# An encoder layer's channel mixer: every engine's order written by hand, right operands summed earlier and split in place

## The chip, the cores and the metric

One core of a Trainium2 chip runs one program. The metric is the device time of one execution in microseconds (us); the profile covers one execution, from the first to the last instruction. The engines are PE (TensorE), ACT (ScalarE), DVE (VectorE), POOL (GpSimd) and SP, whose queue carries every DMA of this kernel.

## The reference

A layer over 2,048 tokens of width 1,024, all in float32:

```
h = rmsnorm(x);  proj = h @ w_in                  # 1024 x 2304
out_a = attention with 8 query heads on 2 key heads, QK-norm, rotary
out_b = differential attention, 4 heads, relative-position bias, then per-head rmsnorm
x = x + concat(out_a, out_b) @ w_out              # 1024 x 1024
h = rmsnorm(x)
u = square(relu(h @ w_up))                        # 1024 x 4096
x = x + u @ w_down                                # 4096 x 1024
```

The last three lines are the channel mixer.

## The kernel before

**Precision.** Each matrix operand is split into a float32r cast (hi, on ACT) and the remainder (lo, on DVE) by `split` (L146, L147). A product is three matmuls: hi hi, hi lo, lo hi.

**Seven products for eight.** Up- and down-projection are each cut 2 x 2 and multiplied with seven half-size products. Each product has a left operand (A11, S2, A12, S3, S1, A22, S4) and a right one (B11, T2, B21, T3, T1, T4, B22). The S and T are sums of quarters, made on POOL by `left_sums` (L709 to L712) and `right_sums` (L718 to L721).

**Output projection** (`out_proj`). w_out comes in eight row blocks through a staging pool of two buffers (`wo_raw`) into eight split tiles that stay. Then for eight blocks of 256 tokens (tc): eight pieces `m_raw` of the attention output are loaded, scaled and split, multiplied with w_out (`py`, L677), added to x and stored as x1. Each 128-token tile is normed: a sum of squares on ACT, a power on POOL (L141), a scaling on DVE, eight transposes on PE. The result `h2_f` is stored to `h2_d` in DRAM.

**Up-projection** (`mlp_up`). For each half c of the tokens (two times 512), `h2_d` is read back in four slices, the T are summed and all seven right operands (128 x 4 x 512, hi and lo, 16 KB of a partition each) are split in 28 slices. Then 16 blocks f of w_up: a 1 MB load, four sums, seven splits (`wu_hi`, `wu_lo`), seven products of 12 matmuls (L763) into three PSUM tiles X, Y, Z. Between them stand p1 (a copy of X on ACT, L784; X is added to only after it), the adds u2, u3, c22, c21, c12 on DVE (L773), and relu and square on ACT (L777, L778). Four sums of the results and seven stores to `us_d` end a block. Three of the right operands lie in a pool (`first`) that is open before the output projection, four in a later one.

**Down-projection** (`mlp_down`). For each of seven products i: 16 pieces of w_down are loaded (one to four loads each), summed in place on POOL (L885) and split into 22 buffers; then for eight token blocks b a tile of u (1 MB) is loaded and split in halves, and 48 matmuls (L899) fill one PSUM tile; `finish` adds it to what it belongs to and stores what is done.

**Memory.** Pools of a stage lie in order of opening from the same base, and a tile waits only for the users of its own bytes. In KB of a partition, attention has: pta 12, acc 8, oa 2, v_a 8, Vb 24, th and tl 8, ob 2, Ka (16) and Ka1 (8) 24, Qa and Qa1 16, Kb 24, T 17.5, Qb 8, Sm 48, small ones. The output projection has: `first` 48, m2b 16, x 8, h 8, gain 4, staging 8, m2a 16, m_raw 7, small 5, w_out 64.

**Order.** A planner simulates the program and orders each engine's instructions, the DMAs on SP's queue among them, from their written priority, its costs and when buffers come free. Engines then run that order without overtaking, waiting on semaphores.

Of the kernel before, what the change touches and what calls it, by code (L numbers as in the profile page):

```python
# [18 lines left out]
P = 128  # L19
# [25 lines left out]
def as32(ap):  # L45
    return ap.bitcast(F32)


class Builder:
# [27 lines left out]
    def dram(self, pool):  # L77
# [8 lines left out]
        self.h2_d = pool.tile([NT, P, ND, P], F32, name="h2_d")  # L86
# [495 lines left out]
    def out_proj(self):  # L582
# [3 lines left out]
        with ExitStack() as es:  # L586
# [4 lines left out]
            stage, m2a, mp, sm = pool("ows", 2), pool("om_a", 1), pool("om", 7), pool("osm", 2)  # L591
# [48 lines left out]
            for tc_ in range(8):  # L640
# [26 lines left out]
                for b in range(NB):  # L667
# [25 lines left out]
                    self.dma(self.h2_d[r0 // P], hf)  # L693
# [21 lines left out]
    def right_sums(self, b11, b12, b21, b22, new):  # L715
# [6 lines left out]
        return {"B11": b11, "T2": t2, "B21": b21, "T3": t3, "T1": t1, "T4": t4, "B22": b22}  # L722

    def mlp_up(self, first):
# [3 lines left out]
        H = 512  # L728
        with ExitStack() as es:
            pool = self.pools(es)  # L730
            later = pool("uh", 1)
            rawp, sump, wop, vp = pool("uraw", 2), pool("usum", 4), pool("uw", 8), pool("uv", 15)
            psx, psy, psz = (pool(n, 2, space=PSUM) for n in ("psux", "psuy", "psuz"))
            for c in range(2):
                B = {}
                for i, n in enumerate(self.RIGHT):
                    B[n] = (first if i < 3 else later).tile([P, 2, 4, H], F32R, name=f"hop_{n}")
                for s in range(4):
                    raw = rawp.tile([P, 2, ND, P], F32, name="h_raw", tag="raw")
                    for i in range(2):  # L740
                        self.dma(raw[:, i], self.h2_d[c * 8 + i * 4 + s])
                    new = lambda: sump.tile([P, 4, P], F32, name="h_sum", tag="sum")
                    blk = lambda i, k: raw[:, k, i * 4 : i * 4 + 4, :]
                    ops = self.right_sums(blk(0, 0), blk(0, 1), blk(1, 0), blk(1, 1), new)
                    ts = slice(s * P, (s + 1) * P)
                    for n in self.RIGHT:
                        self.split(B[n][:, 0, :, ts], B[n][:, 1, :, ts], ops[n])
                for f in range(DFF // 256):
                    raw = rawp.tile([P, ND, 256], F32, name="wu_raw", tag="raw")
                    self.dma(raw, ap["w_up"][0, :, f * 256 : f * 256 + 256].rearrange("(j p) f -> p j f", p=P))  # L750
                    new = lambda: sump.tile([P, 4, P], F32, name="w_sum", tag="sum")
                    blk = lambda i, k: raw[:, k * 4 : k * 4 + 4, i * P : i * P + P]
                    ops = self.left_sums(blk(0, 0), blk(0, 1), blk(1, 0), blk(1, 1), new)
                    A = {}
                    for n in self.LEFT:
                        A[n] = wop.tile([P, 4, P], F32R, name="wu_hi"), wop.tile([P, 4, P], F32R, name="wu_lo")
                        self.split(*A[n], ops[n])

                    def product(ps, i, start):
                        (wh, wl), b = A[self.LEFT[i]], B[self.RIGHT[i]]  # L760
                        for j in range(4):
                            for k, (w, h) in enumerate(((wh, 0), (wh, 1), (wl, 0))):
                                nc.tensor.matmul(  # L763
                                    ps, w[:, j, :], b[:, h, j, :], skip_group_check=not start,
                                    start=(start and j == 0 and k == 0), stop=(j == 3 and k == 2),
                                )

                    def v(name):
                        return vp.tile([P, H], F32, name=name, tag="v")

# [186 lines left out]
```

## Time and profile before

| | |
|---|---|
| Runs | 3445.77, 3447.94 and 8364.44 us; median 3447.94 |
| The profiled execution | 3438.99 us, span 3437.2 us |
| PE busy | 3218.0 us, 94% of the span |
| DVE, ACT, POOL busy | 60%, 45%, 49% |
| DMA | 417.25 MB, mean 121 GB/s |
| Granted clock of PE, mean | 0.972 |

Matmuls are pipelined and their ends are modelled, so PE's busy share says where it has work and not how close it is to its peak. The output projection runs from about 1816 to 2050 us, the up-projection to 2777, the down-projection to the end.

### The profile page before, as it was taken

What the parts mean: (1) busy time and instruction counts of PE and PEld (TensorE: products, weight loads), DVE (VectorE), ACT (ScalarE), POOL (GpSimd) and SP (SyncE); (2) the same over time, 40 slices, a digit from 0 to 9 for tenths busy, and PEclk for the clock granted to TensorE, in tenths of its full rate; (3) what the DMA queues carried; (4) which work ended last, traced back from release to release, by engine and by line L of the source; (5) the groups of instructions that cost most, each with busy time, mean ns of one, the idle gap of its engine ahead of it and who ended that gap; (6) DMA issues with size and microseconds to landing.
All of it is one profiled execution on the core that took longest, in us unless ns stands there. A gap on an engine that the chain in (4) does not pass through costs nothing.

```text
span 3437.2 us, 43470 instructions
## 1 busy us (share of the span) xinstructions
PE 3218.0 (94%) x15584; PEld 2448.7 (71%) x15584; DVE 2065.9 (60%) x3826; ACT 1554.2 (45%) x2386; POOL 1689.7 (49%) x942
## 2 busy tenths in 40 slices
PE   7999989999999999999999986999699979999899
PEld 6888866666666666666666865777577758878787
DVE  6545547777777787777854547445644454454542
ACT  4222227666666656666653224444444433222231
POOL 3434436676666666766661116555655543233600
PEclk9999989999999999999998998999899989999999
DMA  6336380032012211111014543554444477565752
GB/s 200 103 105 206 103 224 22 28 86 59 28 34 74 61 31 44 55 40 29 22 44 165 173 150 119 150 145 138 147 138 138 127 269 253 181 231 191 263 194 86
DMA packets 364408, 417.25 MB, mean 121 GB/s; under 512 B 25344, under 2 KB 293760, under 8 KB 354080
## 3 DMA queue, kind: packets, MB, share of 16 engines
q1 hardware_dynamic: 364192, 414.48, 38.4%
q8 instruction: 123, 2.02, 0.2%
q14 instruction: 93, 0.76, 0.1%
HBM read 283.25 MB, written 139.53 MB: 123 GB/s over the span
## 4 chain that ended last, share of the span: by engine, by line
PE 76%; DVE 11%; DMA 6%; ACT 3%; issue 2%; POOL 1%; SPq 1%; ACTq 0%; POOLq 0%; DVEq 0%
PE pd L899 14%; PE psY L763 7%; PE pq L244 7%; PE po_a L549 6%; PE psX L763 5%; PE py L677 5%; PE ps_s L413 5%; PE psZ L763 5%; PE po_b L467 4%; PE ps_a L538 4%; PE pv L244 3%; PE ps_a L539 3%; PE ptb L460 2%; PE ps_m L503 2%; DVE negm L427 2%
## 5 line engine op out<-in xcount | busy, mean ns | idle before, releaser
L542 POOL TENSOR_TENSOR acc<-acc,pta 128x1024 f32<-128x1024 f32 x224 | 534.1, 2385 | 256.2 <-ACT pta L540 251.4
L418 DVE CUSTOM_DVE_ANT_0 Sm<-ps_s,T 128x512 f32<-128x512 f32 x512 | 338.2, 685 | 124.3 <-PE ps_s L413 122.1
L540 ACT ACTIVATE pta<-ps_a 128x512 f32<-128x512 f32 x512 | 292.2, 594 | 216.2 <-PE ps_a L539 203.3
L899 PE MATMUL pd<-wd_hi,u_hi 128*128 128x512 f32 x896 | 351.3, 392 | 32.6 <-ACT u_hi L146 21.0
L506 DVE TENSOR_REDUCE mxa<-ps_m 128x1 f32<-128x512 f32 x512 | 330.0, 683 | 55.4 <-PE ps_m L503 54.7
L438 POOL TENSOR_TENSOR Sm<-Sm 128x2048 f32<-128x2048 f32 x64 | 293.4, 4584 | 137.5 <-ACT Sm L437 137.4
L899 PE MATMUL pd<-wd_lo,u_hi 128*128 128x512 f32 x896 | 351.0, 392 | 4.2 <-DVE wd_lo L147 4.2
L899 PE MATMUL pd<-wd_hi,u_lo 128*128 128x512 f32 x896 | 350.7, 392 | 1.2 <-DVE u_lo L147 1.2
L413 PE MATMUL ps_s<-Kb,Qb 128*128 128x512 f32 x1024 | 306.1, 409 | 2.6 <-DVE mx L418 2.3
L885 POOL TENSOR_TENSOR wd_raw<-wd_raw 128x512 f32<-128x512 f32 x112 | 182.3, 1640 | 256.1 <-DMA wd_raw<-in_w_down 170.6
L429 ACT ACTIVATE Sm<-Sm,negm 128x2048 f32<-128x2048 f32 x128 | 256.6, 2005 | 88.2 <-DVE negm L427 80.5
L549 PE MATMUL po_a<-pta,v_a 128*64 128x512 f32 x1024 | 280.8, 623 | 2.0 <-ACT pta L540 1.8
L146 ACT CAST u_hi<-u_raw 128x1024 fp32r<-128x1024 f32 x112 | 112.2, 1050 | 326.4 <-PE pd L899 324.0
L538 PEld LDWEIGHTS ps_a<-Qa,Ka 128*128 128x128 f32 x512 | 96.3, 188 | 228.3 <-issue 197.1
L538 PE MATMUL ps_a<-Qa,Ka 128*128 128x512 f32 x512 | 234.1, 458 | 16.4 <-DVE vt L147 12.6
L763 PE MATMUL psX<-hop_B,wu_hi 128*128 128x512 f32 x512 | 166.1, 406 | 88.2 <-ACT wu_hi L146 57.2
L763 PE MATMUL psY<-hop_T,wu_hi 128*128 128x512 f32 x768 | 237.0, 390 | 4.3 <-DVE u L773 4.3
L147 DVE TENSOR_TENSOR tl<-ptb,th 128x512 fp32r<-128x512 f32 x256 | 175.4, 685 | 81.5 <-ACT th L146 81.3
L899 PEld LDWEIGHTS pd<-wd_hi,u_hi 128*128 128x128 f32 x896 | 169.5, 189 | 68.8 <-ACT u_hi L146 21.4
L467 PE MATMUL po_b<-th,Vb 128*128 128x256 f32 x1024 | 208.6, 287 | 9.9 <-ACT th L146 9.4
L413 PEld LDWEIGHTS ps_s<-Kb,Qb 128*128 128x128 f32 x1024 | 179.5, 190 | 47.2 <-DVE mx L418 10.7
L503 PE MATMUL ps_m<-Ka,Qa 128*128 128x512 f32 x512 | 200.8, 432 | 5.8 <-DVE mx L418 1.2
(229 smaller groups left out, 7510.9 us busy)
## 6 DMA issues: line engine op xcount, KB each, us to landing
wd_raw<-in_w_down SPq DMA_DIRECT2D x224, 256.0 KB, 5.5
u_raw<-us_d SPq DMA_DIRECT2D x56, 1024.0 KB, 5.2
wu_raw<-in_w_up SPq DMA_DIRECT2D x32, 1024.0 KB, 6.1
us_d<-us SPq DMA_DIRECT2D x128, 256.0 KB, 5.9
us_d<-c SPq DMA_DIRECT2D x96, 256.0 KB, 2.3
Qb<-qkT_d SPq DMA_DIRECT2D x128, 128.0 KB, 3.0
Qa<-qkT_d SPq DMA_DIRECT2D x48, 256.0 KB, 4.8
m_raw<-mix_d SPq DMA_DIRECT2D x96, 128.0 KB, 2.9
```

Of the source, the lines that this page charges most:

```text
L244: nc.tensor.matmul(ps, a[:, j, :], b[:, j, c0 : c0 + n], start=(j == 0 and k == 0), stop=(j == ND - 1 and k == 2),)
L413: nc.tensor.matmul(ps, Q[:, c, i, qb * P : (qb + 1) * P], K[c][:, ks], start=(i == 0), stop=(i == 1))
L418: nc.vector.tensor_tensor_reduce(out=Sm[:, ks], in0=ps, in1=T[t0][:, o - t0 : o - t0 + 512], scale=1.0, scalar=BIGNEG, op0=ALU.add, op1=AL ...
L438: nc.gpsimd.tensor_tensor(Pm[0], Pm[0], Pm[1], ALU.add)
L467: nc.tensor.matmul(po, V[a][:, kb, :], b[:, kk, :], start=(kb == 0 and n == 0), stop=(kb == NT - 1 and n == 2),)
L506: nc.vector.tensor_reduce(mx[:, kk : kk + 1], ps, AX.X, ALU.max)
L538: nc.tensor.matmul(ps, K[:, ks], Q[:, i, :], start=True, stop=False)
L540: ex = nc.scalar.activation(pt[:, i, :], ps, AF.Exp)
L542: nc.gpsimd.tensor_tensor(acc, prev if kb == 1 else acc, pt, ALU.add)
L549: nc.tensor.matmul(po[i * HD : (i + 1) * HD, :], v_a[:, kb, g * HD : (g + 1) * HD], pt[:, i, :], start=(kb == 0), stop=(kb == NT - 1),)
L763: nc.tensor.matmul(ps, w[:, j, :], b[:, h, j, :], skip_group_check=not start, start=(start and j == 0 and k == 0), stop=(j == 3 and k == 2),)
L899: nc.tensor.matmul(ps, a[:, k, :], w, start=(k == 0 and m == 0), stop=(k == NK - 1 and m == 2))
```

## The change

`h2_d` is replaced by two DRAM tensors, one with the quarters of the normed tokens (`hb_d`) and one with their T sums (`ht_d`); the sums are made tile by tile during the output projection (`mlp_sums`), in raw and sum buffers that are now opened before it. A right operand is then one 1 MB load into its lo half, from which hi is cast and in which the remainder is left (`operand`, `in_place`). The staging pool of w_out has one buffer. Up- and down-projection stand under `manual_schedule`: each engine, SP among them, issues in the written order. Within block n of the up-projection the weights of n + 1 are split, those of n + 2 loaded, and block n - 1 is finished. In the down-projection T2 comes third, each piece of it is also stored (`wt_d`), and T4 is taken from that.

```diff
-        self.h2_d = pool.tile([NT, P, ND, P], F32, name="h2_d")
+        self.hb_d = pool.tile([2, 4, P, 4, 512], F32, name="hb_d")
+        self.ht_d = pool.tile([2, 4, P, 4, 512], F32, name="ht_d")
+        self.wt_d = pool.tile([16, P, 512], F32, name="wt_d")
...
-            stage, m2a, mp, sm = pool("ows", 2), pool("om_a", 1), pool("om", 7), pool("osm", 2)
+            stage, m2a, mp, sm = pool("ows", 1), pool("om_a", 1), pool("om", 7), pool("osm", 2)
...
-                    self.dma(self.h2_d[r0 // P], hf)
+                    c, th, s_ = r0 // 1024, (r0 // 512) % 2, (r0 // P) % 4
+                    for dh in range(2):
+                        self.dma(self.hb_d[c, 2 * dh + th, :, :, s_ * P : s_ * P + P], hf[:, dh * 4 : dh * 4 + 4, :])
+                    if th:
+                        self.mlp_sums(c, s_, rawp, sump)
+                if tc_ == 4:
+                    self.first = [self.operand(0, n, first) for n in self.RIGHT[:3]]
...
+    def mlp_sums(self, c, s, rawp, sump):
+        ts = slice(s * P, s * P + P)
+        raw = rawp.tile([P, 4, 4, P], F32, name="h_raw", tag="raw")
+        for i in range(4):
+            self.dma(raw[:, i], self.hb_d[c, i, :, :, ts])
+        new = lambda: sump.tile([P, 4, P], F32, name="h_sum", tag="sum")
+        for i, t in enumerate(self.right_sums(*(raw[:, i] for i in range(4)), new)):
+            self.dma(self.ht_d[c, i, :, :, ts], t)
...
+    def operand(self, c, n, pool, both=True):
+        t = pool.tile([P, 2, 4, 512], F32R, name=f"hop_{n}")
+        src = (self.hb_d if n[0] == "B" else self.ht_d)[c, self.PLACE[n]]
+        self.dma(t[:, 1], src)
+        if both:
+            self.in_place(t)
+        return t
+    def in_place(self, t):
+        self.split(t[:, 0], t[:, 1], as32(t[:, 1]))
...
+            wop, vp, later = pool("uw", 9), pool("uv", 16), pool("uh", 1)
+            es.enter_context(self.tc.manual_schedule())
...
+            load(0)
+            load(1)
+            sums(0)
+            late = self.RIGHT[3:]
+            for i in range(7):
+                wsplit(0, i)
+                if i >= 3:
+                    B[0][self.RIGHT[i]] = self.operand(0, self.RIGHT[i], later)
+            last = 2 * NF - 1
+            coming = []
+            for n in range(last + 1):
+                if n < last - 1:
+                    load(n + 2)
+                if n < last:
+                    sums(n + 1)
+                if n:
+                    finish(n - 1)
+                X, Y, Z = (p.tile([P, H], F32, name=m) for p, m in ((psx, "psX"), (psy, "psY"), (psz, "psZ")))
+                for i in range(7):
+                    product(n, i, (X, Y, X, Y, Z, Y, Z)[i], i in (0, 1, 4))
+                    if i == 0:
+                        p1 = v("p1")
+                        nc.scalar.copy(p1, X)
+                    elif i == 1:
+                        u2 = add("u2", Y, p1)
+                    elif i == 2:
+                        c11 = act(v("c11"), X)
+                    elif i == 3:
+                        u3 = add("u3", Y, p1)
+                    elif i == 4:
+                        c22 = add("c22", Z, u3)
+                        act(c22, c22)
...
+                    if n < last:
+                        wsplit(n + 1, i)
+
+                    if len(coming) > 2 or (coming and n == NF):
+                        self.in_place(coming.pop(0))
+                    if n == NF - 1:
+                        name = self.RIGHT[i]
+                        B[1][name] = self.operand(1, name, first if i < 3 else later, both=False)
+                        coming.append(B[1][name])
...
+        SPARE = 6
+        order = ("B11", "B21", "T2", "T3", "T1", "T4", "B22")
+        terms = {"B11": "+11", "B21": "+21", "T2": "+12-11-22", "T3": "+22-12", "T1": "+12-11", "T4": "+21-00", "B22": "+22"}
...
+            rp, arp, ap_, bhp, keep, blp, xp = (
+                pool("dr", 10), pool("dar", 2), pool("da", 2), pool("dbh", NK + SPARE), pool("dk", 1), pool("dbl", NK + SPARE), pool("dx", 4),
+            )
...
+            def wsplit(i, k):
+                (t, _), *more = raws.pop((i, k))
+                if order[i] == "T2":
+                    (b, _), (c, _) = more
+                    nc.gpsimd.tensor_tensor(t, t, b, ALU.subtract)
+                    nc.vector.tensor_tensor(t, c, t, ALU.subtract)
+                    self.dma(self.wt_d[k], t)
+                elif more:
+                    nc.gpsimd.tensor_tensor(t, t, more[0][0], ALU.subtract)
+                wh, wl = bhp.tile([P, H], F32R, name="wd_hi"), blp.tile([P, H], F32R, name="wd_lo")
+                self.split(wh, wl, t)
+                Bs[i].append((wh, wl))
...
+            AHEAD = 3
+            made = 0
+            def piece():
+                nonlocal made
+                if made + AHEAD < len(pieces):
+                    wload(*pieces[made + AHEAD])
+                if made < len(pieces):
+                    wsplit(*pieces[made])
+                made += 1
+            uload(0)
+            for q in range(AHEAD):
+                wload(*pieces[q])
+            uload(1)
+            usplit(0)
+            for k in range(NK):
+                piece()
+            for m, (i, b) in enumerate(steps):
+                x = x1(i, b)
+                uload(m + 2)
+                usplit(m + 1)
+                for _ in range(1 if 0 < b < 7 else NK - SPARE if b == 7 else 0):
+                    piece()
+                ps = psd.tile([P, H], F32, name="pd")
...
+                finish(i, b, ps, x)
...
-            with tc.tile_pool(name="mh", bufs=1, reuse_waits="tile") as first:
-                self.out_proj()
-                self.mlp_up(first)
+                first, rawp, sump = pool("uf", 1), pool("uraw", 2), pool("usum", 4)
+                self.out_proj(first, rawp, sump)
+                self.mlp_up(first, rawp, sump)
             self.mlp_down()
```

`first`, the raw buffers and the sum buffers take 48, 16 and 8 KB of a partition; `wop` takes 36, `vp` 32 and `later` 64 KB. In the down-projection the pools in their order take 20, 16, 32, 44, 32, 44 and 8 KB.

## Rows read from the trace of the kernel before

**Rows 1.** windows: us, busy (x) of PE, PEld, DVE, ACT, POOL, PEclk, DMA, GB/s

```profile
1820.00:2045.00 225.00, 219.94 (x1065) 180.47 (x1062) 114.74 (x242) 60.37 (x126) 20.94 (x23) 0.95 0.50 167
2445.00:2777.00 332.00, 312.55 (x1342) 253.52 (x1342) 152.77 (x193) 151.75 (x253) 172.50 (x124) 0.98 0.45 133
2800.00:3437.00 637.00, 616.36 (x2686) 507.05 (x2685) 298.14 (x287) 167.55 (x214) 193.44 (x120) 0.98 0.59 207
```

**Rows 2.** chain of waits, two windows of the up-projection: start us, us, what

```profile
2095.30 2.72 PE psY L763 x12
...
2289.96 0.59 ACT p L784
...
2290.60 3.06 PE psX L763 x12
...
2310.98 1.20 PE psX L763 x4
```

**Rows 3.** waits of PE from 2097 to 2420 us: us in total, times, longest

```profile
PE psX L763 <- ACT p L784: 16.2, 14, 2.6
```

**Rows 4.** timeline into the up-projection: start us, us, instruction

```profile
2044.72 0.40 PE L677 MATMUL py<-wo_hi,m_lo 128*128 128x512 f32 x1
...
2052.59 0.32 SPq L55 DMA_DIRECT2D h_d<-h_f  x1
...
2089.00 1.59 POOL L710 TENSOR_TENSOR w_sum<-w_sum,wu_raw 128x512 f32<-128x512 f32 x1
2089.39 1.75 DVE L147 TENSOR_TENSOR wu_lo<-wu_raw,wu_hi 128x512 fp32r<-128x512 f32 x1
```

**Rows 5.** waits of PE from 2420 to 2450 us

```profile
PE psX L763 <- ACT wu_hi L146: 22.2, 1, 22.2
```

**Rows 6.** waits of PE from 2777 to 2800 us

```profile
PE pd L899 <- ACT u_hi L146: 21.0, 1, 21.0
```

**Rows 7.** chain of waits, 1845 to 1860 us: the last wait for w_out

```profile
1853.39 6.64 PE py L677 x28
```

**Rows 8.** one tile's view, the staging buffers of w_out

```profile
L55 SPq DMA_DIRECT2D wo_raw<-in_w_out x8: 333/333/422, 1816.4 to 1842.9; - x8
L146 ACT CAST wo_hi<-wo_raw x8: 1027/1044/1048, 1821.8 to 1847.4; 128x1024 fp32r<-128x1024 f32 x8
L147 DVE TENSOR_TENSOR wo_lo<-wo_raw,wo_hi x8: 1217/1225/1226, 1822.8 to 1848.5; 128x1024 fp32r<-128x1024 f32 x8
...
DMA to landing us min/median/max: 4.0/5.5/6.1
```

**Rows 9.** one line's view, L413, the last readers of Kb

```profile
L413 PE MATMUL ps_s<-Kb,Qb x1024: 387/396/794, 487.6 to 1732.6; 128*128 128x512 f32 x171
```

**Rows 10.** one line's view, L460 from 1780 to 1800 us

```profile
L460 PE MATMUL ptb<-ident,Sm x20: 271/273/274, 1780.6 to 1796.8; 128*128 128x128 f32 x20
```

**Rows 11.** groups of instructions by line, 2097 to 2777 us

```profile
L147 DVE TENSOR_TENSOR wu_lo<-w_sum,wu_hi 128x512 fp32r<-128x512 f32 x126 | 113.1, 898 | 51.1 <-ACT wu_hi L146 51.0
...
L778 ACT ACTIVATE c<-c 128x512 f32<-128x512 f32 x127 | 80.2, 631 | 3.2
...
L146 ACT CAST wu_hi<-w_sum 128x512 fp32r<-128x512 f32 x124 | 77.0, 622 | 163.1 <-PE psZ L763 70.1 <-PE psY L763 66.0 <-PE psX L763 13.8
...
L773 DVE TENSOR_TENSOR c<-psZ,u 128x512 f32<-128x512 f32 x63 | 43.4, 689 | 47.6 <-PE psZ L763 47.6
...
L718 POOL TENSOR_TENSOR h_sum<-h_raw 128x512 f32<-128x512 f32 x4 | 6.1, 1522 | 5.9 <-DVE wu_lo L147 3.8 <-DVE hop_T L147 1.8 <-DMA h_raw<-h_d 0.3
```

**Rows 12.** DMA issues: bytes of one, median us from issue to landing

```profile
h_d<-h_f SPq DMA_DIRECT2D x16, 512.0 KB, 4.8
h_raw<-h_d SPq DMA_DIRECT2D x16, 512.0 KB, 5.0
```

**Rows 13.** DMA packets and rate from 2777 to 2800 us

```profile
DMA packets 5496, 8.10 MB, mean 352 GB/s; under 512 B 389, under 2 KB 2949, under 8 KB 5240
```

**Rows 14.** the page's costliest groups, the nearest cast of 2048 columns

```profile
L429 ACT ACTIVATE Sm<-Sm,negm 128x2048 f32<-128x2048 f32 x128 | 256.6, 2005 | 88.2 <-DVE negm L427 80.5
```

More of the change, by code (lines that the diff above doesn't have):

```diff
@@ L579, in row_sums, with out_proj @@
         nc.vector.reciprocal(l, l)
[L582 removed]
+    def out_proj(self, first, rawp, sump):
         nc, tc, ap = self.nc, self.tc, self.ap
@@ new lines, in wsplit, with product @@
+            def wsplit(n, i):
+                W[n, i] = wop.tile([P, 4, P], F32R, name="wu_hi"), wop.tile([P, 4, P], F32R, name="wu_lo")
+                self.split(*W[n, i], ops[n][self.LEFT[i]])
+            def product(n, i, ps, start):
+                (wh, wl), b = W[n, i], B[n // NF][self.RIGHT[i]]
+                for j in range(4):
+                    for k, (w, h) in enumerate(((wh, 0), (wh, 1), (wl, 0))):
+                        nc.tensor.matmul(
+                            ps, w[:, j, :], b[:, h, j, :], skip_group_check=not start,
+                            start=(start and j == 0 and k == 0), stop=(j == 3 and k == 2),
+                        )
@@ L806, in mlp_down @@
+            finish(last)
     def mlp_down(self):
@@ L827, in rows, with plus, x1 @@
                 return slice(t0, t0 + P)
-            def x1(half, b, dh):
+            def plus(t, a, b):
+                nc.vector.tensor_tensor(t, a, b, ALU.add)
+            goes = {"B21": (0, 0), "T3": (0, 1), "T1": (1, 1), "T4": (1, 0)}
+            def x1(i, b):
+                if order[i] not in goes:
+                    return None
+                half, dh = goes[order[i]]
                 t = xp.tile([P, H], F32, name="x1")
@@ new lines, in finish @@
+            def finish(i, b, ps, t):
+                n = order[i]
+                if n == "B11":
+                    nc.scalar.copy(U[b], ps)
+                    return
+                if n == "T2":
+                    plus(U[b], ps, U[b])
+                    return
+                if n == "T3":
+                    nc.gpsimd.tensor_tensor(y12[b], t, U[b], ALU.add)
+                    plus(U[b], ps, U[b])
+                    return
+                half, dh = goes.get(n, (0, 1))
+                if n == "B22":
+                    t = y12[b]
+                    plus(t, ps, t)
+                else:
+                    plus(t, ps, t)
+                    plus(t, t, U[b])
+                    if n == "T1":
+                        plus(y12[b], ps, y12[b])
+                self.dma(out[0, rows(half, b), dh * H : dh * H + H], t)
```

206 lines of the change are left out of this document (71 added, 135 removed).

## The prediction

> **What bounds the kernel now.** I read the busy times by stretch first, then TensorE's waits, then the chain of waits where TensorE stops. The change touches three stretches: the output projection, the up-projection and the down-projection. In each, TensorE is busy for over nine tenths and no other engine comes near it [rows 1]. So a saved microsecond must be one in which TensorE waits or runs at half clock. One 128x512 group of 12 matmuls takes 2.72 us; a block n of the up-projection has seven, 19.04 us, and each mlp stage has 2,688 matmuls, 609 us at that pace [rows 2].
>
> What the two mlp stages take beyond 609 us lies in five places:
> - Each n takes 20.38 us (2310.98 less 2290.60), 1.34 more than its matmuls [rows 2]. The wait shown is for the copy p1 [rows 3], which stands on ScalarE behind weight casts that wait for a buffer; without it the group X2 can't add to X.
> - From the last matmul of the output projection (2044.72 + 0.40 = 2045.1, E below) to an undisturbed start (2095.30 - 2.72 = 2092.6): 47.5 us. The right operands are read back, summed and split there, and the sums of VectorE and GpSimd run against one another [rows 4].
> - The same between the halves: 22.2 us in one wait, some 25 with what follows [rows 5].
> - Into the down-projection: 21.0 us [rows 6].
> - Inside the down-projection: 637 less 616 busy, about 21 [rows 1], where a right operand's pieces come late.
> A sixth place lies before them: the output projection runs freely only from 1853.39 [rows 7], after eight blocks of w_out have come through two staging buffers.
>
> **The change part by part.** Negative is saved; the profiled execution took 3438.99 us, and the sum is made against that.
>
> 1. Staging of w_out with one buffer. One at a time, a block costs 5.5 us landing, 1.04 cast and 1.22 remainder, 7.8 us; eight would be 62 us, and from 1816.4, the first load now, full flow would begin 25 us later than it does [rows 8]. But the 24 KB of raw and sum buffers now open ahead of the output projection's pools. By the sizes given above, the staging buffer moves from 84 KB (attention's Ka1 and Qa, read to the end of attention) to 108 KB (Kb, last read at about 1733 [rows 9]), and the w_out tiles to 140 to 204 KB (T, Qb, Sm). The last probabilities in Sm are transposed at 1797 [rows 10], and they may hold back about half the blocks. Four blocks at 6.5 us from 1797 end at 1823; with the loads hidden under attention, full flow begins about 1830. I take -20. Ends: -35 (the first token block's matmuls also fit into attention's tail) and +25 (not free early).
>
> 2. The right operands' sums during the output projection. Added: 32 GpSimd sums of 1.5 us [rows 11], 49 us on an engine busy 21 of 225 [rows 1]; 32 stores and 32 loads of 256 KB and 32 stores of sums in 512-byte pieces on SP; three 1 MB operand loads with three in-place splits. What hides them is that TensorE has its own work. What they can delay is the power for a tile's norm, which queues behind up to four sums (6 us), and loads of m_raw behind a read-back on SP. I take +5, ends 0 and +15.
>
> 3. Into the up-projection. The split of 28 slices falls away, but the last tile's path stays: its store is issued at E + 7.5 [rows 4], lands 4.8 us on and is read back in 5.0 [rows 12], and four sums take 6.1 (four by 1.52): E + 23.5. The second w_up block needs that raw buffer. In the written order of SP, the loads of T3, T1, T4 and B22 stand behind it. The last sum's store (256 KB, half of h_d's 4.8 or so) and four operands of 1 MB at 352 GB/s [rows 13], 12 us, put B22's landing at about E + 38. ScalarE's order puts all four in-place casts ahead of p1 of n = 0; the last cast, of 128x2048, takes 2.0 us by the nearest row [rows 14]. So X2 starts about E + 40.6, as if X0 had started at E + 35. Against 47.5 that is -12. Ends: -36 (the planner gives both w_up blocks their buffers before the last tile needs them) and +5.
>
> 4. The steady up-projection. Weight casts now come one n ahead and in step with the products, so I follow the loop that goes through p1: p1 0.6 [rows 2], three groups 8.16, then for Z4, Y5 and Z6 each an add 0.69, relu and square 1.26 and the next cast 0.62 [rows 11], with a remainder (wu_lo) on VectorE ahead of each of the last two adds. That is 16.5 plus two remainders, plus about 0.5 for some 14 handovers of 0.04. With a remainder of 0.90, the mean [rows 11], the loop is 18.8 us, inside 19.04. One row speaks against the mean: a remainder took 1.75 us beside a sum on GpSimd [rows 4], and then the loop is 20.5. I take a period of 19.15, nearest the mean: 31 times 1.23 is -38. Ends: -41 and +4.
>
> The Trainium skill ("SBUF — State Buffer", "Who interferes with whom") says that a VectorE instruction with two inputs in SBUF and a GpSimd one that reads SBUF exclude each other for a whole instruction. The row of 1.75 agrees: it ends 0.55 us behind the sum's end at 2090.59. If every remainder met a sum, this part would give +4 by that rule and not -38; the rival for it is below.
>
> 5. Between the halves. In SP's order the seven operand loads stand behind the stores of finish(14), whose last waits for GpSimd at about 11 us into n = 15, and each needs its product done. Then a loop runs through the step: add 0.69, relu and square 1.26, weight cast 0.62, in-place cast 2.0, in-place remainder (twice the 1.22 of 1024 columns [rows 8], less what is paid once per instruction: 2.3). That is 6.9 against 2.72, 4.2 lost in a step. Seven such steps would lose 29, three 12.5; the first also waits for its load. I take 23 against 25: -2.
>
> 6. Into the down-projection. Raw pieces and u tiles now lie on operands that the last n frees one after another, up to 16 us before its end, so the first splits run beside its products. About 14 of 21 goes; some pieces share bytes with last results still being stored. Ends: -21 and 0.
>
> 7. Inside the down-projection. T2 becomes third, T4 costs two loads less by its kept sum, but the order now loads three pieces ahead where the planner took what it could. At the switch to T2, seven pieces remain: 21 loads, ten stores and one u tile, 9.2 MB, 26 us at 352 GB/s, against 21 us until the last piece is wanted (10.9 of the running step plus 15 x 0.68). VectorE then does the late finish and u remainders before the next step: 8 to 9 lost. The other three sums lose up to 3.5 each. About 19 in place of 21: I take 0, ends -10 and +15.
>
> The sum is -20 + 5 - 12 - 38 - 2 - 14 + 0 = **-81**: 3438.99 - 81 = 3358. The median of the three runs, 3447.94, is 9 us above the profiled time, so I predict **3367 us**.
>
> **Rivals.**
> - *The written order gives the period back.* If VectorE's remainders regularly meet GpSimd's sums, the loop of part 4 is 20.5 us and the wait for p1 stays: 3367 + 42 = 3409. For it: the row of 1.75, and eight sums plus seven remainders in each n; the in-order ScalarE can't run p1 ahead. Against it: the mean of 0.90, with as many sums in each n now. It decides at a remainder of about 1.0, where the loop reaches 19.04.
> - *The staging gain doesn't come.* If the planner doesn't start w_out under attention, part 1 gives +20 and not -20: 3407. For it: the first load is at 1816 now and Sm lives to 1797; against it: m_raw and the sums of squares, whose buffers lie on Kb, already run in attention's tail.
> - *More overlaps than I count.* Parts 1 and 3 at their near ends: 15 and 24 more: about 3328, down to 3315 with part 7.
> - *Slower than before: SP in the output projection.* Each of eight mlp_sums makes SP wait for a store to land (4.8), then a read-back (5.0), then four sums (6.1) before the sums' stores. Where m_raw loads stand behind these, TensorE waits up to 16 us eight times: +128, 3495. It decides once more than 10 us of each is uncovered. For it: one queue carries every load. Against it: seven m_raw buffers cover up to a token block of 22 us, and the planner, not a written order, places these loads.
>
> **How the numbers follow.** A measurement tells 2% from no change, 69 us, so faster means below 3379. Forecast 0.49 (own range 3325 to 3410), period given back 0.16, staging 0.15, more overlap 0.11, slower 0.09. The range 3305 to 3425 leaves out the slow rival and the corners of the others. Below 3379: 0.41 of the forecast, all of the overlap rival, 0.04 of the next two, 0.56. Above 3517 needs the slow rival with a bad part 4 or 7: 0.05. Within 2%: 0.39.
>
> **What would show it.** After the change I look for the first free-running group of the output projection near 1830; X2 of n = 0 about 40 us after its last matmul; a distance of 19.1 to 19.3 between X0 of neighbouring n, and remainders near 0.9; a loss of 17 to 27 us over n = 15 and 16, spread over several waits for hop tiles; under 10 us between the last product of the up-projection and the first of the down-projection; and the largest wait inside that stage at the switch to T2. A period above 20, a first w_out load after 1810, or m_raw waits in the output projection would make it wrong.

## The result, and the profile after

The changed kernel took **3384.99 us** in the median of four runs (3381.86 to 3395.9), the kernel before 3446.86; the ratio is 0.9834 with a 95% interval from 0.9801 to 0.9866, in which a run of the kernel before of 8364.44 us is left out. That is faster by more than the measurement is uncertain, inside the range of 3305 to 3425, and 18 us above the 3367 forecast. It is a gain of 1.7%, so the 2% that "faster" meant was missed: the prediction had given 0.56 to under 3379 and 0.39 to a change within 2%, which came. The profiled execution has a span of 3384.7 us against 3437.2: 52.5 us less, where the sum of the parts said 81.

The stages of the two profiled executions, each from its first or to its last matmul (start: the first product of block n = 1 less 19.04 us; for the kernel before as in the prediction):

| | before | after | change | forecast |
|---|---|---|---|---|
| output projection ends (E; parts 1, 2) | 2045.1 | 2059.6 | +14.5 | -15 |
| E to the undisturbed start (part 3) | 47.5 | 46.1 | -1.4 | -12 |
| start to the last product (parts 4, 5) | 684.8 | 635.2 | -49.6 | -40 |
| to the first matmul of the down-projection (part 6) | 21.0 | 4.8 | -16.2 | -14 |
| down-projection (part 7) | 635.0 | 635.3 | +0.3 | 0 |

The busy times by stretch; columns as in [rows 1]. The first row is the changed kernel's output projection from its 96th matmul on; the second and third are 260 us of steady blocks in the second half of the up-projection, before and after:

```profile
1865.00:2060.00 195.00, 182.17 (x864) 146.89 (x863) 96.84 (x180) 45.29 (x92) 39.60 (x38) 0.97 0.69 219
...
2480.00:2740.00 260.00, 247.85 (x1079) 201.31 (x1078) 117.92 (x153) 121.58 (x203) 139.31 (x102) 1.00 0.48 139
...
2460.00:2720.00 260.00, 260.00 (x1149) 215.29 (x1148) 134.45 (x165) 122.77 (x216) 161.46 (x109) 1.00 0.52 151
```

In the up-projection TensorE is busy for 260.00 of 260 us, where it was for 247.85 before. In the first row it misses 13 us of 195, and the DMA moves 219 GB/s. The chain of waits of the changed kernel shows the pace of the up-projection (start us, us, what):

```profile
2455.32 2.72 PE psX L789 x12
...
2474.36 1.81 PE psX L789 x8
```

From X0 of one block to that of the next are 19.04 us (2474.36 less 2455.32), exactly seven products. The waits of TensorE (us in total, times, longest us) in three stretches: the first half, the step between the halves, and the way into the down-projection:

```profile
PE psX L789 <- ACT p L837: 10.5, 1, 10.5
PE psY L789 <- DVE u L799: 1.6, 1, 1.6
...
PE psZ L789 <- DVE c L799: 7.9, 1, 7.9
PE psX L789 <- ACT p L837: 6.1, 1, 6.1
PE psY L789 <- DVE u L799: 3.7, 2, 2.1
...
PE pd L1001 <- ACT wd_hi L149: 4.8, 1, 4.8
PE pd L1001 <- DVE wd_lo L150: 0.8, 1, 0.8
```

The wait for p1 of [rows 3] is gone from the steady blocks. What is left is one wait for p1 and one for a late sum in the first block of the first half, four waits of 17.7 us in all between the halves, and 5.6 us where [rows 6] had 21.0.

### The profile page after: what moved, and what is told of

It is laid out like the page before. It is cut to its first block, busy times and chain, and to the rows that moved or that the text cites. A ratio compares the mean times of both kernels' runs of the same rounds, so it can differ in the third digit from the quotient of the medians.

```text
span 3384.7 us, 43164 instructions
## 1 busy us (share of the span) xinstructions
PE 3227.7 (95%) x15584; PEld 2459.7 (73%) x15584; DVE 2042.2 (60%) x3800; ACT 1530.4 (45%) x2344; POOL 1631.6 (48%) x894
## 5 line engine op out<-in xcount | busy, mean ns | idle before, releaser
L541 PE MATMUL ps_a<-Qa,Ka 128*128 128x512 f32 x512 | 233.6, 457 | 17.7 <-DVE vt L150 13.6
L470 PEld LDWEIGHTS po_b<-th,Vb 128*128 128x128 f32 x1024 | 173.1, 191 | 44.0 <-ACT th L149 14.7
L1001 PEld LDWEIGHTS pd<-wd_lo,u_hi 128*128 128x128 f32 x896 | 169.5, 189 | 48.9 <-DVE wd_lo L150 14.2
L1001 PEld LDWEIGHTS pd<-wd_hi,u_hi 128*128 128x128 f32 x896 | 169.4, 189 | 46.4 <-ACT wd_hi L149 11.3
```

The lines of the kernel that those rows point to most:

```text
L470: nc.tensor.matmul(po, V[a][:, kb, :], b[:, kk, :], start=(kb == 0 and n == 0), stop=(kb == NT - 1 and n == 2),)
L541: nc.tensor.matmul(ps, K[:, ks], Q[:, i, :], start=True, stop=False)
L1001: nc.tensor.matmul(ps, a[:, k, :], w, start=(k == 0 and q == 0), stop=(k == NK - 1 and q == 2))
```

## The experiments

All edits are to the changed kernel except where the kernel before is named. Seen over the runs that left a stage as it was, the end of the output projection lies between 2057 and 2063 us and the written down-projection between 634 and 640; a difference of under 6 us there isn't read. Before, after and the last row of the table ran several times, the others once. The stage times, in the table's order except that here the up-projection counts from its first matmul (X0), which exists in every order:

| kernel | E | E to X0 | X0 to last product | to next stage | down | span |
|---|---|---|---|---|---|---|
| before | 2045.1 | 41.7 | 690.6 | 21.0 | 635.0 | 3437.2 |
| after | 2059.6 | 29.5 | 651.8 | 4.8 | 635.3 | 3384.7 |
| before, nine weight buffers | 2046.0 | 41.9 | 656.2 | 21.0 | 641.5 | 3410.5 |
| planner in the up-projection | 2063.1 | 38.7 | 634.8 | 3.9 | 638.7 | 3382.9 |
| planner in the down-projection | 2063.3 | 26.3 | 652.9 | 7.0 | 619.1 | 3372.8 |
| half blocks, three staging buffers | 2047.2 | 27.6 | 653.9 | 4.7 | 639.8 | 3377.0 |
| no right sums | 2054.3 | 11.2 | 657.0 | 4.7 | 634.2 | 3365.7 |
| late operands first | 2060.8 | 39.1 | 642.2 | 4.7 | 635.6 | 3386.3 |
| second w_up block last | 2060.6 | 27.6 | 664.1 | 4.7 | 639.0 | 3399.7 |
| first splits after the seventh token block | 2057.5 | 28.7 | 652.4 | 4.6 | 638.7 | 3385.8 |
| first splits at the head of the up-projection | 2062.9 | 27.9 | 655.5 | 6.6 | 637.3 | 3393.8 |
| splits between halves later | 2057.3 | 27.7 | 681.6 | 4.7 | 639.3 | 3414.4 |
| combined | 2054.5 | -0.2 | 642.2 | 3.7 | 647.5 | 3351.5 |
| combined, planner in the down-projection | 2056.2 | -0.2 | 641.5 | 3.7 | 629.2 | 3334.3 |

**What gave the period: the order?** The up-projection without its written order:

```diff
             psx, psy, psz = (pool(n, 2, space=PSUM) for n in ("psux", "psuy", "psuz"))
-            es.enter_context(self.tc.manual_schedule())
```

> The up-projection's written order is left to the planner, all else as in the changed kernel. Theory (the written order, with the weights split one block ahead in step with the products, is what brought a block from 20.4 to 19.04 us): the period goes back to 20.0 to 20.5 with waits for p1, the span grows by 30 to 45 us. Rival (the sums made earlier and the in-place splits did it, the order doesn't matter): the period stays at 19.04 to 19.2 and the span within 12 us.

The rival's numbers held: the steady blocks of the planner's order are 19.04 us apart too, with one wait for p1 from 2120 to 2400 us:

```profile
PE psX L788 <- ACT p L836: 5.9, 1, 5.9
```

My theory fell. From E to the last product the planner even took 673.5 us for the written order's 681.3. Between the halves it waits less (2400 to 2470 us):

```profile
PE psX L788 <- ACT p L836: 2.9, 1, 2.9
PE psZ L788 <- DVE c L798: 1.2, 1, 1.2
```

Its four blocks around the step lose 15.3 us for 25.8; its last two lose 6.9, where the written order loses 0.2. The rival's reason, the earlier sums and the in-place splits, is not shown by this run, and the next one speaks against it.

**Or a buffer?** The changed kernel has nine pairs of buffers for split weights where there were eight. This one edit to the kernel before:

```diff
-            rawp, sump, wop, vp = pool("uraw", 2), pool("usum", 4), pool("uw", 8), pool("uv", 15)
+            rawp, sump, wop, vp = pool("uraw", 2), pool("usum", 4), pool("uw", 9), pool("uv", 15)
```

> The kernel before with one edit: nine buffers instead of eight for the split w_up weights, the planner's order kept. Leaving the changed kernel's order to the planner did not bring the old period back, so the order is not the cause. Theory (the copy p1 waited on ScalarE behind weight casts that waited for a buffer; the ninth buffer lets the cast start): the period falls from 20.4 to 19.0 to 19.5, the up-projection is 27 to 40 us shorter. Rival (the place of the splits in the code, a block ahead and between the products, gives it, by the planner's priorities too): the period stays at 20.2 or more.

The theory held. The chain of waits, from X0 of one block to the next:

```profile
2205.28 2.72 PE psX L763 x12
...
2224.32 2.72 PE psX L763 x12
...
2243.36 2.72 PE psX L763 x12
```

19.04 us (2224.32 less 2205.28, 2243.36 less 2224.32), with the planner's order, the old sums and the old splits. The stage is 34.4 us shorter. Counted by 84 matmuls in the order in which TensorE ran them, 31.8 of these are 24 blocks that took 20.35 to 20.39 us and take 19.04 here, as they do in the changed kernel. One run took 3412.68 us beside 3452.84 for the kernel before. So the ninth buffer is enough in the planner's order; whether the written order would have done it with eight no run shows.

**The output projection: the cast that waits.** From 1860 us to the end of this stage the changed kernel's TensorE has one wait of over 2 us. The timeline of it (start us, us, instruction, in brackets the idle time before and what ended it):

```profile
1985.08 1.90 ACT L149 CAST hop_T<-hop_T 128x2048 fp32r<-128x2048 f32 x1 [8.17 <-DMA hop_T<-ht_d]
1986.88 0.71 ACT L149 CAST m_hi<-m_raw 128x256 fp32r<-128x256 f32 x2
...
1987.33 0.80 PE L680 MATMUL py<-wo_hi,m_hi 128*128 128x512 f32 x1 [6.12 <-ACT m_hi L149]
```

ScalarE stands at the in-place cast of T2 for 8.17 us until its load has landed; the cast of m_raw that TensorE needs is behind it. A first attempt to move it:

```diff
-                    self.first = [self.operand(0, n, first) for n in self.RIGHT[:3]]
+                    self.first = [self.operand(0, n, first, both=False) for n in self.RIGHT[:3]]
+                if tc_ == 6:
+                    for t in self.first:
+                        self.in_place(t)
```

> The three first right operands are still loaded after the fifth token block of the output projection, but cast and left with their remainder only after the seventh. In the changed kernel 48 matmuls near 1990 us took 22.6 us where the kernel before needed 12.6, with one wait of 6.1 us for a cast of m_raw and half clock after it. Theory (an in-place cast stands on ScalarE ahead of that cast and waits for its 1 MB load): the wait is gone, the last matmul of the output projection ends near 2050 instead of 2059.6, the span is 8 to 11 us shorter. Rival (the transfers and the sums themselves, on the queue and on GpSimd, delay m_raw): the last matmul stays within 2 us of 2059.6.

It decided nothing: the planner put the cast in the same place (8.58 us of idle time before it at 1983.24, 6.9 us of wait). The next one writes the splits at the head of the up-projection, which moved the cast on ScalarE (4.89 us of idle time before it at 1985.51):

> The in-place splits of the first three right operands are written at the head of the up-projection; their loads stay after the fifth token block. The planner still puts the casts into the output projection, but that of T2, the one that waited 8.2 to 8.6 us for its load at 1983 us, some fifteen instructions of ScalarE later. Theory (that cast, waiting on the in-order ScalarE, made the wait of 6 to 7 us for m_hi): the 48 matmuls near 1990 us take 13 to 15 us instead of 22.6, the output projection ends near 2050. Rival (m_raw itself comes late): its end stays at 2057 to 2061.

The waits of TensorE from 1860 us to the end of the stage:

```profile
PE py L680 <- ACT m_hi L149: 1.7, 1, 1.7
...
PE pt L166 <- DVE xo L161: 7.3, 3, 4.3
```

The wait for m_hi fell from 6.1 to 1.7 us, and the stage ended at 2062.9, no sooner: other waits, for the normed tile above all, took its place. The theory fell; the rival had the end nearly right, but no row shows its reason, an m_raw that comes late. So a single visible wait wasn't the cost.

**The output projection: the sums.** The sums and their read-back left out, as many bytes stored:

```diff
-                        self.mlp_sums(c, s_, rawp, sump)
+                        for i in range(4):
+                            self.dma(self.ht_d[c, i, :, :, s_ * P : s_ * P + P], hf[:, (i % 2) * 4 : (i % 2) * 4 + 4, :])
```

> The right operands' sums are left out: no read-back and no sums on GpSimd in the output projection; as many bytes of the normed tokens are stored in the sums' place, so the operands' values are wrong and all later work is the same. Theory (the sums and their read-back cost the output projection its 14.5 us over the kernel before, and hold the raw buffers into which w_up is loaded): the output projection ends at 2045 to 2051 instead of 2059.6, and the undisturbed start of the up-projection follows 20 to 30 us behind it instead of 46. Rival (the operand loads and the last tile's norm set both): the end stays above 2055 and the distance above 40.

E came at 2054.3, between the two. But its 96th matmul began late (1871.5; 1865.1 in the changed kernel and in the kernel before). From there to the end it took 182.8 us, against 194.5 with the sums (194.4 to 196.4 in the runs that left this stage as it was) and 180.0 before: by this run the sums and their read-back cost 11.7 of the 14.5 us. The start of the up-projection followed 33.2 us behind E, between the two again. X0 was there at 11.2, so the round trip of the last sums is what holds it up. But then the fourth product waited for a sum on VectorE:

```profile
PE psY L790 <- DVE u L800: 13.6, 1, 13.6
```

What VectorE did before that sum:

```profile
2077.13 0.69 DVE L150 TENSOR_TENSOR wu_lo<-w_sum,wu_hi 128x512 fp32r<-128x512 f32 x1 [9.48 <-DMA ht_d<-h_f]
...
2092.17 0.68 DVE L800 TENSOR_TENSOR u<-psY,p 128x512 f32<-128x512 f32 x1
```

A remainder of the weights waited 9.48 us for a store of `h_f`; by the sizes, the weights' buffers (72 to 108 KB) lie over those of `h_f` (96 to 104 KB). The four in-place remainders came behind it, all ahead of the sum in VectorE's written order. The stores from `h_f` to `ht_d` are this edit's own, so part of the 13.6 us may belong to the experiment.

**Staging.** Half blocks of w_out through three buffers, and not whole blocks through one:

```diff
-            stage, m2a, mp, sm = pool("ows", 1), ...
+            stage, m2a, mp, sm = pool("ows", 3), ...
...
-                raw = stage.tile([P, D], F32, name="wo_raw")
+                for q in range(2):
+                    raw = stage.tile([P, 512], F32, name="wo_raw")
...
```

> The staging of w_out takes half blocks in three buffers (6 KB of a partition) instead of whole blocks in one (4 KB). In the changed kernel two blocks came early, the others were held by attention's last probabilities until 1801 us and then came one at a time, 6 to 7.5 us each, until 1848; the kernel before started later with two buffers and ended at the same time. Theory (the depth of one, from 1801 on, ate the early start): the last remainder of w_out ends at 1825 to 1835, and the first 96 matmuls of the output projection, done at 1865 in both kernels, are done 10 to 18 us sooner, as is its end. Rival (VectorE and ScalarE, still busy with attention until 1822, set the pace): under 4 us.

The staging tiles of the changed kernel and of this one (op, count, duration min/median/max in ns, first and last start):

```profile
L55 SPq DMA_DIRECT2D wo_raw<-in_w_out x8: 333/333/419, 1731.2 to 1840.8; - x8
L149 ACT CAST wo_hi<-wo_raw x8: 1039/1046/1049, 1742.4 to 1845.3; 128x1024 fp32r<-128x1024 f32 x8
```

```profile
L55 SPq DMA_DIRECT2D wo_raw<-in_w_out x16: 328/333/430, 1731.6 to 1823.7; - x16
L149 ACT CAST wo_hi<-wo_raw x16: 607/619/640, 1742.0 to 1827.1; 128x512 fp32r<-128x512 f32 x16
```

The last cast moved from 1845.3 to 1827.1, the 96th matmul from 1865.1 to 1847.8, the end from 2059.6 to 2047.2. The theory held. 5 of the 17 us are lost again before the end, in part to work that has moved: 44 small matmuls of the sums of squares now come behind the 96th, and none did in the changed kernel.

**Into the up-projection: the order of the loads.** Two orders on SP: the four late operands ahead of both w_up blocks, and between the two.

```diff
+            late = self.RIGHT[3:]
+            for name in late:
+                B[0][name] = self.operand(0, name, later)
             load(0)
             load(1)
```

> The four late right operands are loaded and split ahead of the first two blocks of w_up in the written order. Theory (X2 of the first block waited for in-place casts whose loads stood behind the second w_up block): X2 follows the second product at once, the undisturbed start, 46.1 us after the last matmul of the output projection in the changed kernel, comes 13 to 17 us sooner. Rival (the 4 MB delay the first w_up block by as much, 12 us at 352 GB/s): the first product starts about 40 us after that matmul instead of 29.5, the gain is under 4 us.

```diff
             load(0)
+            for name in late:
+                B[0][name] = self.operand(0, name, later, both=False)
             load(1)
```

> On the DMA queue the four late right operands are loaded between the first and the second w_up block, not behind the second. Theory (only the second block waits for the buffer of the last sums, issued at 2087.4 us, so the operands were held up by 8 us): X0 of the first block starts where it did, 29.5 us after the last matmul of the output projection, the in-place casts and p1 come 7 to 9 us sooner, and the undisturbed start 46.4 us after it comes at 37 to 40. Rival (the operands wait for memory that the output projection still holds, as their loads ahead of everything did): the first block is not delayed but the operands are no sooner, the start stays at 45 to 47.

In the first, X0 came 39.1 us behind E and the undisturbed start at 46.1, as in the changed kernel: the rival held. In the second the start came at 55.1, worse than either expected. Its DMA queue, and the sum on GpSimd that was late:

```profile
2082.52 0.62 SPq L55 DMA_DIRECT2D hop_B<-hb_d  x1
2083.23 12.48 SPq L55 DMA_DIRECT2D ht_d<-h_sum  x3
2095.76 1.46 SPq L55 DMA_DIRECT2D wu_raw<-in_w_up  x1
...
2100.59 1.26 POOL L719 TENSOR_TENSOR w_sum<-w_sum,wu_raw 128x512 f32<-128x512 f32 x1 [8.42 <-DMA ht_d<-h_sum]
```

The operands were issued by 2083.1, and the issue of three of the last sums' stores behind them took until 2095.7. Until such a store has landed, its buffer isn't free for a sum of the weights: GpSimd waited 8.42 us for that, and ScalarE 13.71 for that sum. In both orders the 4 MB only pushed something else back.

**Between the halves: start the splits later?**

```diff
-                    if len(coming) > 2 or (coming and n == NF):
+                    if len(coming) > 5 or (coming and n == NF):
```

> The in-place splits of the second half's operands start three products later (when five are in the queue instead of two). Theory (the first of them stands on ScalarE and VectorE before its load has landed, and what the product needs is behind it): the wait of 7.9 us in the first half's last block and the half clock after it go, the loss over the two blocks falls from 26 to 14 to 18 us, the span by 8 to 12. Rival (the seven splits are more work than the products cover, 4.2 us each beside 2.72): the loss stays at 22 or more and only moves into the next block.

The theory fell. The rival was right that the loss moves into the next block and stays above 22, but neither expected that it would double: in the last block of the first half it went from 10.6 to 5.5 us, and in the next from 15.2 to 48.1. The waits there:

```profile
PE psY L789 <- ACT hop_T L149: 11.1, 3, 4.4
PE psX L789 <- ACT hop_B L149: 5.3, 1, 5.3
PE psX L789 <- DVE hop_B L150: 5.1, 2, 3.4
```

Now each split is written right behind the product before the one that uses it, where three products stood between, and each product waits for its own: cast, then remainder.

**The written order of the down-projection.**

```diff
             psd = pool("psd", 4, space=PSUM)
-            es.enter_context(self.tc.manual_schedule())
```

> The down-projection's order is left to the planner, all else as in the changed kernel. Theory (the written order of the DMA queue and the casts brings the first pieces and the first u tile beside the last block's products, which took the way into the stage from 21.0 to 4.8 us): it goes back to 14 to 21 us; inside the stage, 635 us, nothing changes by over 6. Rival (the new order of the pools frees the bytes early, whoever orders): it stays under 8 us.

The way in stayed short (7.0), so the written order of this stage isn't what gave part 6. The rival's reason, the pools' new order, is what is left; no run changed it by itself. And the stage became 16.2 us shorter, which neither expected. After its first product, 96.7, each of the planner's products takes 87.0 to 87.2 us for 384 matmuls; the only waits:

```profile
PE pd L1000 <- ACT wd_hi L149: 11.2, 2, 7.0
PE pd L1000 <- DVE wd_lo L150: 0.2, 1, 0.2
```

In the written order the first, the third (T2) and the sixth (T4) took 94.2, 101.8 and 91.0. At the switch to T2, in the changed kernel, TensorE makes eight waits of 0.4 to 1.3 us, 6.0 in all, and the rest of the 14.8 us goes with the clock: 0.67 of full speed in the mean of this stretch, so part of it at 1.2 GHz and part at 2.4.

```profile
2929.00:2955.00 26.00, 19.69 (x52) 11.32 (x50) 17.68 (x18) 5.90 (x9) 13.24 (x9) 0.67 0.95 334
```

**Combined.** Staging as above; the normed tile written to `h2_f` and not over x1; the second half's sums made in the up-projection's blocks 1 to 8, in place, in a buffer of 4 KB (v buffers 14 for 16); the late operands each in a pool of its own over what the output projection frees first, split in the first block behind p1; in block 15 the operand loads ahead of the stores, and the cast of an operand ahead of the activations.

```diff
+            flat = out.rearrange("p j t -> p (j t)")
+            nc.vector.scalar_tensor_tensor(flat, xt, r, gain, op0=ALU.mult, op1=ALU.mult)
...
-                    if th:
+                    if th and not c:
...
+            hop = {n: pool("uh" + n, 1) for n in ("T3", "B22", "T1", "T4")}
+            vp, hx, wop = pool("uv", 14), pool("ux", 1), pool("uw", 9)
...
+                if 1 <= n <= 8:
+                    hq = hload(n - 1)
...
+                    if t is not None and i > 3:
+                        nc.scalar.copy(t[:, 0], as32(t[:, 1]))
...
```

> A version from the findings so far: staging as in the run above; the normed tile written beside x1 and not over it, so that it doesn't wait for x1's store; the sums of the second half made during the first eight blocks of the up-projection, in place in a buffer of their own, so that w_up isn't held up behind them; the four late operands in pools over the memory that the output projection frees first, split behind p1 inside the first block; in the last block of the first half the operand loads ahead of the stores, and a cast ahead of the activations that it waited behind. Theory: the output projection ends 15 to 25 us sooner than in the changed kernel, the undisturbed start follows 5 to 15 us behind it instead of 46, the two halves lose 12 to 18 us instead of 26: the span is 55 to 85 us shorter, 3300 to 3330. Rival (the late operands' loads, w_up and the last stores share the transfers, so the start is as late as their 6 MB, 18 us at 352 GB/s, and the splits need): the start follows 25 to 30 us behind, the span is 35 to 50 us shorter.

The start came 19.0 us behind E, between theory and rival, and the halves lost 13.5 instead of 25.8. The span is 33.2 us shorter, less than either expected. The output projection ended only 5.1 us sooner: from its 96th matmul it took 205.2 us, against 199.5 with the three buffers alone, and why isn't shown. The down-projection grew by 12, by one wait of 13.3 us. The chain there:

```profile
2706.01 1.27 POOL us L724
...
2709.41 3.58 DMA us_d<-us
...
2713.56 0.70 DVE wd_lo L150
```

A remainder of w_down waits until the up-projection's last sums are stored. I take it that it is written over them, since the smaller v pool has moved; no run puts the pool back. With the planner's order in the down-projection:

> The version above with the down-projection's order left to the planner, one edit. The stage took 647.5 us there, with one wait of 13.3 us for a remainder of w_down, 635.3 in the changed kernel, and 619.1 with the planner's order. Theory (each stage's time adds up, the order of the down-projection depends only on that stage): 617 to 625 us in the stage, 4 to 8 us on the way into it, the span 3318 to 3332, the ratio to the kernel before 0.960 to 0.968. Rival (the written order was slow by what preceded it, not by itself, or the planner moves the earlier stages too): the stage stays above 630, the span above 3335.

Median **3335.53 us** of four runs (3332.55 to 3340.02), ratio to the kernel before 0.9683, interval 0.9667 to 0.9699, faster than the kernel before and the changed kernel. The stage took 629.2, between theory and rival, since the wait is there whoever orders; its first product took 106.8 us, the other six 87.0 to 87.2 each:

```profile
PE pd L1048 <- DVE wd_lo L150: 15.7, 1, 15.7
```

## Why the prediction was right in size, and where it was not

**1, staging: failed.** Forecast -20, measured 0: the 96th matmul came at 1865.1 in both. The place of the buffer was right, and two blocks were loaded early (1731 and 1750). The step "they may hold back about half the blocks. Four blocks at 6.5 us from 1797 end at 1823" failed: only one block was cast early (1742.4). The second waited until 1801.7, and six more followed 5.8 to 9.2 us apart, the last at 1845.3. The rival of the staging gain that doesn't come had the right side, though the loads did start early. That the depth of one is what the early start was lost to is shown by the run with three buffers, whose 96th matmul came 17.3 us sooner.

**2, sums: mis-sized.** Forecast +5 within 0 to +15, measured +14.5; the run without sums puts 11.7 on them. What they use up stays open: the wait for the T2 cast was visible, and taking most of it away gained nothing. TensorE's waits for m_hi (6.1 us) and m_raw (1.3), which the prediction named as a sign that it is wrong, came. Against the same stretch of the kernel before, the DMA moves 219 GB/s and not 153, and TensorE has more waits and a granted clock of 0.97 and not 1.00:

```profile
1865.00:2045.00 180.00, 179.44 (x893) 148.20 (x891) 89.50 (x191) 41.77 (x91) 15.11 (x18) 1.00 0.45 153
```

**3, into the up-projection: mis-sized.** Forecast -12, measured -1.4. The timeline of the changed kernel:

```profile
2059.20 0.40 PE L680 MATMUL py<-wo_hi,m_lo 128*128 128x512 f32 x1
...
2074.65 0.60 SPq L55 DMA_DIRECT2D hb_d<-h_f  x1
...
2087.39 1.01 SPq L55 DMA_DIRECT2D wu_raw<-in_w_up  x1
...
2097.68 1.90 ACT L149 CAST hop_T<-hop_T 128x2048 fp32r<-128x2048 f32 x1 [3.51 <-DMA hop_T<-ht_d]
...
2105.14 1.90 ACT L149 CAST hop_B<-hop_B 128x2048 fp32r<-128x2048 f32 x1
2106.94 0.58 ACT L837 COPY p<-psX 128x512 f32<-128x512 f32 x1
...
2107.58 1.22 PE L789 MATMUL psX<-hop_B,wu_hi 128*128 128x512 f32 x2 [10.47 <-ACT p L837]
```

The last tile's store was issued at E + 15.1 and not at E + 7.5; what follows it took 12.7 us and not 16, so that the second w_up block was issued at E + 27.8 and not E + 23.5. The first late operand was cast at E + 38.1, where I had put the last one's landing. And I counted one cast of 2.0 us ahead of p1, where four of 1.90 stand in a row with weight casts between them: 9.3 us from 2097.68 to p1 at 2106.94. X2 began at E + 48.0, not E + 40.6.

**4, the period: right in size, unpriced in cause.** The block takes 19.04 us for a forecast of 19.15. But only 24 blocks ran at 20.35 to 20.39 before, not 31, so 31.8 us are saved for a forecast of 38. The place was right (p1 "stands on ScalarE behind weight casts that wait for a buffer"). The reason given for its going, casts that the written order puts one n ahead, was not needed: the ninth buffer, which I didn't cost, is enough without it. The rival that gives the period back needed remainders of 1.0 us; they took 0.96 in the mean ((52.2 + 46.4) / 103):

```profile
L150 DVE TENSOR_TENSOR wu_lo<-w_sum,wu_hi 128x512 fp32r<-128x512 f32 x59 | 52.2, 884 | 56.1 <-ACT wu_hi L149 56.1
...
L150 DVE TENSOR_TENSOR wu_lo<-wu_raw,wu_hi 128x512 fp32r<-128x512 f32 x44 | 46.4, 1055 | 63.6 <-ACT wu_hi L149 63.6
```

**5, between the halves: right in size, wrong in what it replaces.** The two blocks lose 25.8 us for a forecast of 23, and loads behind the stores of the block before are part of it: the first in-place remainder waited 8.73 us for its cast, which waited for its load. The waits are not for the operands themselves, as I expected, but for results (c, p1, u) that stand behind the splits on ScalarE and VectorE. They are 17.7 us; the rest goes with the clock, which the sum had not counted:

```profile
2405.00:2455.00 50.00, 32.28 (x109) 24.55 (x108) 30.29 (x22) 24.69 (x28) 19.78 (x11) 0.80 0.60 216
```

What was off is the old price. Counted by 84 matmuls as above, the four blocks around the step lost 37.1 us before and not 25, and the last two blocks of the stage lost 6.8, where they now lose 0.2; the sum had no term for these. Parts 4 and 5 together gave 9.6 more than forecast: 6 less in the period, 9 more between the halves, 6.7 at the end.

**6** was right in size (-16.2 for -14). Its reason, that u tiles and pieces lie on bytes freed early, agrees with the planner's order keeping the way in short, but was not tested by itself. **7** was right in its sum only: the switch to T2 lost 14.8 for 8 to 9, and the written order has 16 us that the planner's doesn't.

So 29.5 us too hopeful before the up-projection, 10.6 at its start, 11.5 too careful behind: 52.4 saved for 81. That the errors have opposite signs, and so leave the total within the range, is luck. (The low end of the overlap rival was added up wrongly: 3328 less 10 is 3318, not 3315.)

## What to carry to other kernels

A rewrite that changes order, buffers and places at once is costed by which wait each of them ends: here one more buffer for the split weights, a one-digit edit, alone took 34 us off the up-projection, and the written order of the down-projection cost 16. When tiles are loaded while an earlier stage still runs, count how many of them lie on bytes that stage holds to its end, and price the rest by the staging depth. An in-place cast on an in-order engine is late for everything behind it as soon as its load is; price all that stand in a row, not the last. And moving one such cast away gains nothing where the next wait stands close behind, as in the output projection here.

## What the hardware showed that I had not expected

A remainder on VectorE and a sum on GpSimd that meet don't run side by side here: one waits for the other's end. From between the halves of the changed kernel, the last row a remainder with no sum beside it:

```profile
2441.06 1.75 POOL L721 TENSOR_TENSOR us<-c,us 128x512 f32<-128x512 f32 x1
...
2441.57 3.38 DVE L150 TENSOR_TENSOR hop_T<-hop_T 128x2048 fp32r<-128x2048 f32 x1
...
2442.76 3.34 POOL L718 TENSOR_TENSOR w_sum<-wu_raw 128x512 f32<-128x512 f32 x1
...
2412.72 2.29 DVE L150 TENSOR_TENSOR hop_B<-hop_B 128x2048 fp32r<-128x2048 f32 x1 [8.73 <-ACT hop_B L149]
```

The remainder of 2048 columns ended 2.14 us after the first sum (2444.95 less 2442.81), which is about what it takes alone, 2.29; the second sum ended 1.15 us after the remainder (2446.10), and such a sum takes 1.26 to 1.30 alone. So some 1.2 of the 3.38 us and 2.2 of the 3.34 are waiting. This is what the Trainium skill ("SBUF — State Buffer", "Who interferes with whom") says of such a pair, and the trace agrees. How much of part 2 it makes is not shown.
